# Transposes of gated retention tokens by pairs in one two-bank PSUM tile, with a new order around them and more products of ones at both ends

## The chip, the cores and the metric

The kernel runs on one core of a Trainium2 chip. The metric is the device time of one execution in microseconds (us). The kernel before was run three times: 1474.34, 1474.58 and 1475.74 us, median 1474.58. Lower is better.

## What is computed

The reference is one inference step of a decoder with two layers: layer 0 mixes tokens by a short gated convolution, layer 1 by multi-scale retention with four heads; each mixer is followed by a SwiGLU feed-forward layer, and a last RMS norm ends the step. There are 512 prompt tokens of one sequence and 32 sample tokens (8 sequences of 4), 544 in all, each of 1024 numbers, everything in fp32. The part that the change touches is retention:

```
z = x @ w_in                      # q, k (256 a head), v, g (512 a head)
q, k = rotary(q), rotary(k) / 16
per chunk: o = (q k^T * decay) v + (q S) * cross_w      # S: 256 x 512 state of a head
           S = S * chunk_decay + (k * state_w)^T v
o = (o - mean(o)) / sqrt(var(o) + eps) * gn_g           # per token and head
out = (silu(g) * o) @ w_out
```

and the last norm:

```
y = x / sqrt(mean(x * x) + eps) * final_norm
```

The outputs are y of both groups and the new convolution and retention states.

## The kernel before, in words

**Layout and precision.** Activations lie with features on the 128 partitions and the 544 tokens along the free dimension. Each fp32 operand is split into a high and a low part (xh and xl, wh and wl; ACT makes the high part at L185, DVE the low part at L186), and a product is the sum of three: high by high, low by high, high by low. `project` (L164 to 181, its matmul at L172) does this for one weight tile, eight k's of 128 and two halves of 272 tokens: 48 matmuls of 128x272. `mm3` (L160 to L162) does the same for the attention products.

**PSUM.** There are two pools. `psum()` hands out one of two tiles of two banks each (named mm in the profile), `bank()` one of four tiles of one bank (sm). A tile comes back to the pool when its last reader is done, and the instruction that takes it next waits for that reader. Dependencies are kept by tile.

**Order.** Instructions are issued to each engine in the order of the code, with due places set by `tc.issue_after(ins)`: what stands in that block goes behind the named instruction in the order. `last_product[0]` holds the last matmul of `project`, `mm3` or the sample products. Where two steps stand side by side a scheduler mixes them.

**A head of retention** (the loop over h, L1162 on). After values, gates, scores and states, for each of the four token tiles `inner` (L1043) makes the tile's attention output in a bank, from the middle state (mid by qk) and the scores (vh, vl by sh, sl), and `normalized` (L1031) brings it to group norm: statistics (L1036, L1037), the root by POOL (L219, L220), and yn = (pt − mean) · rs on DVE (L1040). `sample_outputs` (L1096, products at L1104) multiplies the sample queries by one of four pieces of the sample states S, loaded by `states_load` through SP's queue; `states_update` (L1109, four products at L1120 into two two-bank tiles, two DVE multiplications at L1125, then a store of S) brings the piece up to date. `gated` (L1060) transposes yn by four TensorE transposes (L1064) into a bank and multiplies the gate tile by it on DVE (L1067; L1071 for the sample tokens). `out_project` (L1128) splits the gated tokens into yh and yl and multiplies them by the output weights.

In heads 0 to 2, the rotated q and k of the next head are made meanwhile: `qk_project(h + 1, nxt, 1, 0)` and so on, each one `project` and its rotation on DVE (L866, L872 to L877). The order there is: the first of these projections; sample outputs of piece 3 and `inner` of tile 3; then `gated` of yn0 and yn1 (each with a bank of its own); normalisations of tile 2 and of the sample tokens (yns); the state update of piece 2; the second projection, with the state update of piece 3 and `gated` of yn2 inside it; normalisation of tile 3; `gated` of yns and of yn3; the last two projections and the output projection.

Head 3 has no next head. There two of the four gate projections are put late: `gate_project(3, 2)` with the state update of piece 2 inside, the sample outputs of piece 3, `gate_project(3, 3)` with the state update of piece 3 inside, then `gated` of yn0, yn1 and yn2 one behind the other, `inner` of tile 3, `gated` of yns, normalisation of tile 3 and the output projection, which takes `gated` of yn3 between two of its parts.

**The start.** While the first weights arrive, TensorE multiplies a tile of ones by itself (WARM = 7 times, L298).

**The last norm** (`final`, L698). The last three feed-forward output tiles are made for the first half of the tokens and then for the second; squares are summed (ACT at L210 and L214, DVE at L211 and L215), `scale` makes the means by three matmuls (L729), takes the root on POOL (L731) and spreads it over the partitions by three matmuls (L224). `gained` multiplies x by the norm's gains on ACT (L721), `out` multiplies by the spread root (L746 or POOL; R is a copy of it by ACT, L742) and stores. Three products of ones stand behind the sums of the second half (L765).

Of the kernel before, what the change touches and what calls it, by code (L numbers as in the profile page):

```python
# [9 lines left out]
AF = mybir.ActivationFunctionType  # L10
ALU = mybir.AluOpType

P = 128
D = 1024
KT = D // P
# [17 lines left out]
NVEC = 80  # L33
LATE = 3
LEAD = 3
WARM = 7

MADE = [0, 4, 2, 6, 3, 7, 1, 5]
RD = [(r, dt) for r in range(2) for dt in range(2)]
# [7 lines left out]
def hybrid_decode_kernel(ctx: ExitStack, tc: tile.TileContext, a: dict, o: dict):  # L47
    nc = tc.nc
# [26 lines left out]
    def bank():  # L75
        return ps.tile([P, 512], F32, tag="sm", name=nm("sm"), bufs=4)
# [16 lines left out]
    ident = cb[:, 544 : 544 + P]  # L93
    mean_w = cb[:, 672 : 672 + P]
# [19 lines left out]
    def g_fin(kt):  # L114
        return vec[:, 72 + kt : 73 + kt]
# [41 lines left out]
    last_product = [None]  # L157
# [64 lines left out]
    def spread(out, tt, lo, hi):  # L222

        return nc.tensor.matmul(  # L224
            out, rN[:, tt : tt + 1].to_broadcast([P, P]), ident[:, lo:hi], start=True, stop=True, skip_group_check=True
        )
# [471 lines left out]
    def final(ms, acts, group_weights, fp, tp):  # L698

        ah, al = acts  # L700
        ws = [group_weights(n, ms) for n in range(KT - LATE, KT)]

        sums = {}

        def products(hf):
            c = slice(hf * HT, (hf + 1) * HT)
            for n in range(KT - LATE, KT):
                wh, wl = ws[n - KT + LATE]
                pt = [None, None]
                pt[hf] = bank()  # L710
                project(pt, wh, wl, 0, ah, al, hfs=(hf,))
                nc.vector.tensor_add(x[n][:, c], x[n][:, c], half(pt, hf)[:, :HT])
                square_sum(n, tp, "gu", 4, c=c, add=nc.vector)
                yield

        def gained(hf):

            c = slice(hf * HT, (hf + 1) * HT)
            y = [fp.tile([P, 4, HT], F32, tag="f", name=nm("ya")), tp.tile([P, 4, HT], F32, tag="gu", name=nm("yb"))]
            for kt in range(KT):  # L720
                last_gain[0] = nc.scalar.activation(y[kt // 4][:, kt % 4, :], x[kt][:, c], AF.Copy, scale=g_fin(kt))  # L721
            return y

        def scale(hf):
            pt = bank()
            mq = pt[:, 496:499]
            for i, at in enumerate((0, P, HT - P)):
                cols = slice(hf * HT + at, hf * HT + at + P)
                last_sum[0] = nc.tensor.matmul(mq[:, i : i + 1], sqacc[:, cols], mean_w[:, 0:1], start=True, stop=True)  # L729
            nc.vector.tensor_scalar_add(rN[:, :3], mq, EPS)  # L730
            nc.gpsimd.tensor_tensor(rN[:, :3], rN[:, :3], expo[:, :3], op=ALU.pow)  # L731
            yield
            for i, (lo, hi) in enumerate(((0, P), (0, P), (3 * P - HT, P))):
                spread(pt[:, i * P : i * P + hi - lo], i, lo, hi)
            sums[hf] = pt[:, :HT]

        def out(hf, y, w):

            yy = y[w // 2][:, w % 2 * 2 : w % 2 * 2 + 2, :]
            if w == 0:  # L740
                with tc.issue_after(last_square[0].ins):
                    nc.scalar.activation(R[:, hf, :], sums[hf], AF.Copy)  # L742
                for i in range(2):
                    nc.gpsimd.tensor_tensor(yy[:, i, :], yy[:, i, :], R[:, hf, :], op=ALU.mult)
            else:
                nc.vector.tensor_mul(yy, yy, sums[hf].unsqueeze(1).to_broadcast([P, 2, HT]))  # L746
            q = nc.sync if w % 2 else nc.scalar
            q.dma_start(o["yT"][hf][:, 2 * w : 2 * w + 2], yy)

        last_gain, last_sum = [None], [None]  # L750
        drain(products(0))
        first, second = scale(0), products(1)
        next(second)
        next(first)
        y0 = gained(0)
        drain(second)
        drain(first)
        out(0, y0, 0)
        out(0, y0, 1)
        rest = scale(1)  # L760
        next(rest)
        with tc.issue_after(last_sum[0].ins):
            wm = bank()
            for _ in range(3):
                nc.tensor.matmul(wm[:, :P], ones, ones, start=True, stop=True)  # L765
        y1 = gained(1)
        out(0, y0, 2)
        out(0, y0, 3)
        drain(rest)
        for w in range(4):  # L770
            out(1, y1, w)
# [4 lines left out]
    with ExitStack() as c2:  # L776
# [37 lines left out]
        def token_tiles(tt):  # L814
            return slice(tt * P, (tt + 1) * P)
# [35 lines left out]
        def qk_project(h, st, which, dt, inside=None):  # L851

            wh, wl = load_piece(a["rtqk"][h, which * 2 + dt], KT * P)
            pt = [bank(), bank()] if inside else psum()
            if inside:
                project(pt, wh, wl, 0, xh, xl, last=False, ks=range(KP))
                inside()
                project(pt, wh, wl, 0, xh, xl, first=False, ks=range(KP, KT))
            else:
                project(pt, wh, wl, 0, xh, xl)  # L860
            qk_rotate(st, which, dt, pt)
# [195 lines left out]
                )  # L1057
            return pt

        def gated(h, st, yn, it):  # L1060

            pt = bank()
            for n in range(4):
                nc.tensor.transpose(pt[:, token_tiles(n)], yn[:, token_tiles(n)], ident)  # L1064
            if it < 4:
                gs = st["gate"][:, :, token_tiles(it)]
                nc.vector.tensor_mul(gs, gs, pt.rearrange("p (n t) -> p n t", n=4))  # L1067
            else:
                gs = st["gate"][:, :, SEQ:].rearrange("p n (g c) -> p n g c", g=4)
                ys = pt.rearrange("p (n g c) -> p n g c", n=4, g=4)[:, :, :, 0:8]  # L1070
                nc.vector.tensor_mul(gs, gs, ys)  # L1071

        def sample_scores(h, st):

# [87 lines left out]
        for h in range(NH):  # L1162
            more = h + 1 < NH
            value(h, st)
            st["S"] = {}
            for i in range(3):
                states_load(h, st, i)
            gate_project(h, st, 0)
            sample_operands(h, st)
            state(h, st, 0)  # L1170
            gate_project(h, st, 1)
            state(h, st, 1)
            for c in range(2):
                scores(h, st, c)
            if more:
                gate_project(h, st, 2)
                gate_project(h, st, 3)
            sample_outputs(h, st, 0)
            states_update(h, st, 0)
            states_load(h, st, 3)  # L1180
            yn0 = normalized(inner(h, st, 0))
            sample_outputs(h, st, 1)
            yn1 = normalized(inner(h, st, 1))
            states_update(h, st, 1)
            sample_outputs(h, st, 2)
            p2 = inner(h, st, 2)
            if more:
                nxt = qk_start(h + 1)
                for which in (1, 0):
                    qk_scale(nxt, which)  # L1190
                with tc.issue_after(last_product[0].ins):
                    qk_project(h + 1, nxt, 1, 0)
                sample_outputs(h, st, 3)
                p3 = inner(h, st, 3)
                with tc.issue_after(last_product[0].ins):
                    gated(h, st, yn0, 0)
                    gated(h, st, yn1, 1)
                yn2 = normalized(p2)
                yns = normalized(st["po"])
                states_update(h, st, 2)  # L1200

                def inside():
                    states_update(h, st, 3)
                    gated(h, st, yn2, 2)

                qk_project(h + 1, nxt, 1, 1, inside)
                yn3 = normalized(p3)
                gated(h, st, yns, 4)
                gated(h, st, yn3, 3)
                qk_project(h + 1, nxt, 0, 0)  # L1210
                qk_project(h + 1, nxt, 0, 1)
                out_project(h, st)
            else:
                yn2 = normalized(p2, "gt")
                gate_project(h, st, 2, lambda: states_update(h, st, 2))
                sample_outputs(h, st, 3)
                yns = normalized(st["po"], "rot1")
                gate_project(h, st, 3, lambda: states_update(h, st, 3))
                for it, yn in enumerate((yn0, yn1, yn2)):
                    gated(h, st, yn, it)  # L1220
                p3 = inner(h, st, 3)
                gated(h, st, yns, 4)
                yn3 = normalized(p3)
                out_project(h, st, [lambda: None, lambda: gated(h, st, yn3, 3)])
            st = nxt
# [121 lines left out]
```

## Time and profile before

| what | value |
|---|---|
| median of three runs | 1474.58 us (1474.34 to 1475.74) |
| the profiled execution's own time | 1474.22 us |
| span of its instructions | 1472.4 us |
| matmuls on TensorE | 11002 |
| DMA | 172.83 MB, mean 117 GB/s |
| mean granted clock of TensorE | 0.997 |

The profile is of one execution. Engines are PE (TensorE's matmuls), PEld (its weight loads, which lie beside PE), DVE (VectorE), ACT (ScalarE), POOL (GpSimd) and SP (SyncE, which issues most DMAs). A row of a time line has the start in us, the duration, the engine, the line of the kernel, the operation, output <- inputs by the program's names, the shape and the count (x4: four instructions taken together); in brackets stands how long the engine had been idle before, and what ended that. In the rows of waits, the numbers are the total in us, the number of times and the longest. fp32 matmuls (transposes, products of ones) leave two records each where the fp32r matmuls of the projections leave one; for transposes the profile shows one. The ends of matmuls are modelled, so distances are better read from start to start. The clock granted to TensorE is given as a share of full speed.

### The profile page before, as it was taken

What the parts mean: (1) busy time and instruction counts of PE and PEld (TensorE: products, weight loads), DVE (VectorE), ACT (ScalarE), POOL (GpSimd) and SP (SyncE); (2) the same over time, 40 slices, a digit from 0 to 9 for tenths busy, and PEclk for the clock granted to TensorE, in tenths of its full rate; (3) what the DMA queues carried; (4) which work ended last, traced back from release to release, by engine and by line L of the source; (5) the groups of instructions that cost most, each with busy time, mean ns of one, the idle gap of its engine ahead of it and who ended that gap; (6) DMA issues with size and microseconds to landing.
All of it is one profiled execution on the core that took longest, in us unless ns stands there. A gap on an engine that the chain in (4) does not pass through costs nothing.

```text
span 1472.4 us, 25982 instructions
## 1 busy us (share of the span) xinstructions
PE 1457.5 (99%) x11002; PEld 1388.6 (94%) x11002; DVE 921.2 (63%) x1397; ACT 572.4 (39%) x821; POOL 82.7 (6%) x107
## 2 busy tenths in 40 slices
PE   9999999999999999999999999999999999999997
PEld 9999999999999999897987988898799999999997
DVE  5645439847748647648545834844759847748645
ACT  5222355625525335242142224114265625525434
POOL 0100220000000003000000000000030000000002
PEclk9999999999999999999999999999999999999998
DMA  6222274232322326337235513714564232322322
GB/s 223 82 93 86 89 175 112 91 103 89 100 93 88 100 65 192 105 115 249 82 115 186 187 45 118 267 44 135 180 154 109 94 104 89 105 93 88 101 65 83
DMA packets 69748, 172.83 MB, mean 117 GB/s; under 512 B 6512, under 2 KB 23792, under 8 KB 69632
## 3 DMA queue, kind: packets, MB, share of 16 engines
q1 hardware_dynamic: 66576, 162.01, 33.5%
q0 software_dynamic: 2192, 7.94, 3.3%
q8 instruction: 86, 1.41, 0.4%
q10 hardware_dynamic: 864, 1.22, 0.2%
q14 instruction: 30, 0.25, 0.0%
HBM read 149.97 MB, written 21.18 MB: 116 GB/s over the span
## 4 chain that ended last, share of the span: by engine, by line
PE 95%; DVE 2%; DMA 2%; ACT 0%; POOL 0%; issue 0%; DVEq 0%; POOLq 0%; ACTq 0%; SPq 0%
PE mm L172 42%; PE sm L458 26%; PE sm L172 13%; PE sm L898 2%; PE sm L899 2%; PE sm L900 2%; PE sm L160 1%; PE sm L162 1%; PE sm L161 1%; DMA S<-in_rets_dram 1%; PE sm L1104 1%; DVE S L1125 1%; PE mm L905 1%; DVE yn L1040 0%; PE sm L224 0%; PE mm L1120 0%
## 5 line engine op out<-in xcount | busy, mean ns | idle before, releaser
L185 ACT ACTIVATE wh<-w 128x1024 fp32r<-128x1024 f32 (+4 forms) x215 | 209.9, 980 | 454.8 <-PE mm L172 269.4
L186 DVE TENSOR_TENSOR wl<-w,wh 128x1024 fp32r<-128x1024 f32 (+4 forms) x215 | 243.1, 1135 | 44.2 <-ACT wh L185 40.9
L172 PE MATMUL mm<-xh,wh 128*128 128x272 f32 x1060 | 221.7, 290 | 0.3 <-ACT wh L185 0.3
L172 PE MATMUL mm<-xl,wh 128*128 128x272 f32 x1060 | 219.5, 288 | 0.0
L172 PE MATMUL mm<-xh,wl 128*128 128x272 f32 x1060 | 219.5, 289 | 0.0
L172 PEld LDWEIGHTS mm<-xh,wh 128*128 128x128 f32 x1060 | 166.3, 189 | 5.4 <-DVE wl L186 3.4
L172 PEld LDWEIGHTS mm<-xl,wh 128*128 128x128 f32 x1060 | 166.6, 189 | 0.0
L458 PE MATMUL sm<-oh,wh 128*128 128x272 f32 x576 | 166.6, 289 | 0.0
L458 PE MATMUL sm<-oh,wl 128*128 128x272 f32 x576 | 166.5, 289 | 0.0
L458 PE MATMUL sm<-ol,wh 128*128 128x272 f32 x576 | 166.2, 289 | 0.0
L172 PEld LDWEIGHTS mm<-xh,wl 128*128 128x128 f32 x1060 | 165.7, 189 | 0.4
L266 DVE TENSOR_TENSOR x<-x,mm 128x544 f32<-128x544 f32 x85 | 61.2, 720 | 145.5 <-PE mm L172 145.5
L458 PE MATMUL sm<-oh,l 128*128 128x272 f32 x432 | 124.8, 289 | 0.0
L458 PE MATMUL sm<-ol,h 128*128 128x272 f32 x432 | 124.7, 289 | 0.0
L458 PE MATMUL sm<-oh,h 128*128 128x272 f32 x432 | 124.7, 289 | 0.0
L458 PEld LDWEIGHTS sm<-oh,wh 128*128 128x128 f32 x576 | 108.6, 189 | 0.6 <-ACT u L515 0.6
L458 PEld LDWEIGHTS sm<-oh,wl 128*128 128x128 f32 x576 | 108.7, 189 | 0.0
L458 PEld LDWEIGHTS sm<-ol,wh 128*128 128x128 f32 x576 | 108.5, 188 | 0.0
L186 DVE TENSOR_TENSOR l<-w,h 128x1024 fp32r<-128x1024 f32 x72 | 68.8, 956 | 55.5 <-ACT h L185 55.3
L172 PE MATMUL mm<-xh,f 128*128 128x272 f32 x576 | 99.3, 288 | 0.0
L172 PE MATMUL sm<-xh,wh 128*128 128x272 f32 x412 | 90.2, 292 | 0.7 <-DVE yn L1040 0.5
L172 PE MATMUL sm<-xh,wl 128*128 128x272 f32 x412 | 87.8, 288 | 0.0
(264 smaller groups left out, 2863.2 us busy)
## 6 DMA issues: line engine op xcount, KB each, us to landing
w<-in_ffgu_dram SPq DMA_DIRECT2D x88, 512.0 KB, 3.5
w<-in_ffdn_dram SPq DMA_DIRECT2D x96, 192.0 KB, 2.5
S<-in_rets_dram SPq DMA_DIRECT2D x16, 1024.0 KB, 7.1
out_rets_dram<-S SPq DMA_DIRECT2D x16, 1024.0 KB, 4.8
w<-in_cvin_dram SPq DMA_DIRECT2D x21, 512.0 KB, 3.5
w<-in_rtqk_dram SPq DMA_DIRECT2D x16, 512.0 KB, 3.7
w<-in_rtv_dram SPq DMA_DIRECT2D x16, 512.0 KB, 3.6
w<-in_rtg_dram SPq DMA_DIRECT2D x16, 512.0 KB, 3.9
```

The source lines that it names most:

```text
L160: nc.tensor.matmul(out, lh, rh, start=start, stop=False, skip_group_check=True)
L161: nc.tensor.matmul(out, lh, rl, start=False, stop=False, skip_group_check=True)
L162: last_product[0] = nc.tensor.matmul(out, ll, rh, start=False, stop=stop, skip_group_check=True)
L172: last_product[0] = nc.tensor.matmul(half(pt, hf)[:, :HT], w[:, c], act[k][:, hf * HT : (hf + 1) * HT], start=(first and k == ks[0] and i ...
L185: h = nc.scalar.activation(dh, src, AF.Copy)
L186: nc.vector.tensor_sub(dl, src, dh.bitcast(F32))
L266: last_residual[0] = nc.vector.tensor_add(xk, xk, p)
L458: nc.tensor.matmul(out, w[:, c], b[k][:, at, :], start=(first and k == 0 and i == 0), stop=(k == n - 1 and i == 2), skip_group_check=True,)
L898: nc.tensor.matmul(out, xh[kt][:, ts_], wh[:, cw], start=(kt == 0), stop=False)
L899: nc.tensor.matmul(out, xh[kt][:, ts_], wl[:, cw], start=False, stop=False)
L900: nc.tensor.matmul(out, xl[kt][:, ts_], wh[:, cw], start=False, stop=(kt == KT - 1))
L905: nc.tensor.matmul(pvs[g * NS : (g + 1) * NS, 0, :], xs[:, kt, :], raw[kt // 2][:, kt % 2 * DV : (kt % 2 + 1) * DV], start=(c == 1), stop= ...
```

## The change

1. `WARM` goes from 7 to 8.
2. `gated` can be given a tile. `gated_pair` takes one two-bank tile by `psum()` and lets two `gated` write its two halves. The transposes now also set `last_product[0]`.
3. Heads 0 to 2: `gated` of yn0 and yn1 become a pair and move ahead of the sample outputs of piece 3 and of `inner` of tile 3, right behind the first projection. `gated` of yns and yn3 become a pair.
4. Head 3: the sample outputs of piece 3 move, with the state update of piece 3, to the inside of the last gate projection; the normalisation of the sample tokens comes behind that projection; yn0 and yn1 become a pair, yn2 keeps a bank.
5. The last norm: four products of ones behind the spreads of the first half, the sums of the second half behind these, five products of ones (before: three) behind the sums. The last two gains of the second half are issued behind the last square.

```diff
-WARM = 7
+WARM = 8
...
             for kt in range(KT):
-                last_gain[0] = nc.scalar.activation(y[kt // 4][:, kt % 4, :], x[kt][:, c], AF.Copy, scale=g_fin(kt))
+                with tc.issue_after(last_square[0].ins) if hf and kt == KT - 2 else ExitStack():
+                    nc.scalar.activation(y[kt // 4][:, kt % 4, :], x[kt][:, c], AF.Copy, scale=g_fin(kt))
...
+        def idle(n, ins):
+
+            with tc.issue_after(ins):
+                wm = bank()
+                for _ in range(n):
+                    last_spread[0] = nc.tensor.matmul(wm[:, :P], ones, ones, start=True, stop=True)
...
+        idle(4, last_spread[0].ins)
         rest = scale(1)
-        next(rest)
-        with tc.issue_after(last_sum[0].ins):
-            wm = bank()
-            for _ in range(3):
-                nc.tensor.matmul(wm[:, :P], ones, ones, start=True, stop=True)
+        with tc.issue_after(last_spread[0].ins):
+            next(rest)
+        idle(5, last_sum[1].ins)
         y1 = gained(1)
...
-        def gated(h, st, yn, it):
+        def gated(h, st, yn, it, pt=None):
 
-            pt = bank()
+            pt = bank() if pt is None else pt
             for n in range(4):
-                nc.tensor.transpose(pt[:, token_tiles(n)], yn[:, token_tiles(n)], ident)
+                last_product[0] = nc.tensor.transpose(pt[:, token_tiles(n)], yn[:, token_tiles(n)], ident)
...
+        def gated_pair(h, st, *pair):
+            pt = psum()
+            for i, (yn, it) in enumerate(pair):
+                gated(h, st, yn, it, pt[:, i, :])
...
                     qk_project(h + 1, nxt, 1, 0)
+                with tc.issue_after(last_product[0].ins):
+                    gated_pair(h, st, (yn0, 0), (yn1, 1))
                 sample_outputs(h, st, 3)
                 p3 = inner(h, st, 3)
-                with tc.issue_after(last_product[0].ins):
-                    gated(h, st, yn0, 0)
-                    gated(h, st, yn1, 1)
...
-                gated(h, st, yns, 4)
-                gated(h, st, yn3, 3)
+                gated_pair(h, st, (yns, 4), (yn3, 3))
...
                 gate_project(h, st, 2, lambda: states_update(h, st, 2))
-                sample_outputs(h, st, 3)
+
+                def inside():
+                    sample_outputs(h, st, 3)
+                    states_update(h, st, 3)
+
+                gate_project(h, st, 3, inside)
                 yns = normalized(st["po"], "rot1")
-                gate_project(h, st, 3, lambda: states_update(h, st, 3))
-                for it, yn in enumerate((yn0, yn1, yn2)):
-                    gated(h, st, yn, it)
+                gated_pair(h, st, (yn0, 0), (yn1, 1))
+                gated(h, st, yn2, 2)
```

The order in which the instructions of the changed program stand on each engine: in heads 0 to 2 PE has, behind the first projection, the four transposes of yn0, five products of `inner` of tile 3, the four transposes of yn1, the four sample products of piece 3, the other seven products of `inner`, the four products of the state update of piece 2, 24 projection products, the four of piece 3, the transposes of yn2, 24 projection products, the transposes of yns, 19 projection products and the transposes of yn3. On DVE the gate multiplication by yn0 stands right behind the first rotation (L866), then the normalisation of tile 2 and the gate multiplication by yn1. PE has seven instructions more than before (10840 for 10833), all products of ones.

More of the change, by code (lines that the diff above doesn't have):

```diff
@@ L728, in scale @@
                 cols = slice(hf * HT + at, hf * HT + at + P)
-                last_sum[0] = nc.tensor.matmul(mq[:, i : i + 1], sqacc[:, cols], mean_w[:, 0:1], start=True, stop=True)
+                last_sum[hf] = nc.tensor.matmul(mq[:, i : i + 1], sqacc[:, cols], mean_w[:, 0:1], start=True, stop=True)
             nc.vector.tensor_scalar_add(rN[:, :3], mq, EPS)
@@ L733, in scale @@
             for i, (lo, hi) in enumerate(((0, P), (0, P), (3 * P - HT, P))):
-                spread(pt[:, i * P : i * P + hi - lo], i, lo, hi)
+                last_spread[0] = spread(pt[:, i * P : i * P + hi - lo], i, lo, hi)
             sums[hf] = pt[:, :HT]
@@ L748, in out @@
             q.dma_start(o["yT"][hf][:, 2 * w : 2 * w + 2], yy)
-        last_gain, last_sum = [None], [None]
+        last_sum, last_spread = {}, [None]
+        def idle(n, ins):
[3 more added lines that the diff above has]
+                    last_spread[0] = nc.tensor.matmul(wm[:, :P], ones, ones, start=True, stop=True)
         drain(products(0))
```

## The prediction

> **What bounds the kernel now.** I read the page first (busy times, then the chain that ended last), then PE's waits, then the time line of PE and DVE around the code that the change touches.
>
> ```profile
> span 1472.4 us, 25982 instructions
> PE 1457.5 (99%) x11002; PEld 1388.6 (94%) x11002; DVE 921.2 (63%) x1397; ACT 572.4 (39%) x821; POOL 82.7 (6%) x107
> PE 95%; DVE 2%; DMA 2%; ACT 0%; POOL 0%; issue 0%; DVEq 0%; POOLq 0%; ACTq 0%; SPq 0%
> ```
>
> TensorE (PE) is busy for 1457.5 of 1472.4 us and makes up 95% of the chain. The change removes no product of the model, so it can win only where PE stands still or runs at a lower clock, about 15 us. This view of PE's waits names such places:
>
> ```profile
> PE sm L1104 <- DMA S<-in_rets_dram: 1.6, 2, 1.0
> PE sm L1064 <- DVE gate L1067: 1.5, 3, 0.5
> PE sm L1064 <- DVE yn L1040: 1.4, 4, 0.4
> PE sm L729 <- DVE sqacc L211: 1.2, 2, 1.0
> PE sm L172 <- DVE yn L1040: 0.5, 3, 0.2
> ```
>
> (After the arrow the releaser; then the total in us, how often, the longest.) The transposes of gated tokens (L1064) and what follows them wait 1.5 + 1.4 + 0.5 = 3.4 us, the sample products (L1104) 1.6 us for their state's DMA, the last sums (L729) 1.2 us. The change aims at these; 1474.22 us is the profiled execution, 1.8 us of it outside the span.
>
> A 0.2% change is 2.95 us, about what a measurement of this kernel can tell from none. The shown runs' median, 1474.58, lies 0.36 above the profiled execution and their spread is 1.40; I add no correction for it.
>
> **Heads 0 to 2.** Head 0 on PE, then on DVE (start, duration, line; in brackets the idle time before and what ended it):
>
> ```profile
> 677.01 0.40 PE L160 MATMUL sm<-mid,qkh 128*128 128x512 f32 x1
> 677.25 0.39 PE L161 MATMUL sm<-mid,qkh 128*128 128x512 f32 x1
> ...
> 680.97 0.60 PE L1064 MATMUL sm<-cb,yn 128*128 128x128 f32 x4
> 681.49 0.51 PE L1120 MATMUL mm<-vs,kns 32*128 32x512 f32 x4
> 682.51 0.66 PE L1064 MATMUL sm<-cb,yn 128*128 128x128 f32 x4 [0.51 <-DVE gate L1067]
> 683.32 0.37 PE L172 MATMUL sm<-xh,wh 128*128 128x272 f32 x1 [0.15 <-DVE yn L1040]
> ...
> 686.51 0.51 PE L1120 MATMUL mm<-vs,kns 32*128 32x512 f32 x4
> 686.95 0.39 PE L172 MATMUL sm<-xh,wh 128*128 128x272 f32 x1
> 687.18 0.60 PE L1064 MATMUL sm<-cb,yn 128*128 128x128 f32 x4
> 687.53 0.37 PE L172 MATMUL sm<-xh,wh 128*128 128x272 f32 x1
> ...
> 690.49 0.60 PE L1064 MATMUL sm<-cb,yn 128*128 128x128 f32 x4
> 690.85 0.50 PE L172 MATMUL mm<-xh,wh 128*128 128x272 f32 x2
> ...
> 691.86 0.66 PE L1064 MATMUL sm<-cb,yn 128*128 128x128 f32 x4 [0.40 <-DVE yn L1040]
> ```
>
> ```profile
> 677.22 0.72 DVE L866 TENSOR_TENSOR rot<-mm,gt 128x544 f32<-128x544 f32 x1 [4.02 <-PE mm L172]
> ...
> 681.78 0.67 DVE L1067 TENSOR_TENSOR gate<-gate,sm 128x512 f32<-128x512 f32 x1
> 682.37 0.81 DVE L1040 TENSOR_SCALAR yn<-sm,mv,rs 128x512 f32<-128x512 f32 x1
> ...
> 683.90 1.19 DVE L1125 SCALAR_TENSOR_TENSOR S<-S,mm 128x1024 f32<-128x1024 f32 x1
> ...
> 685.07 1.21 DVE L1125 SCALAR_TENSOR_TENSOR S<-S,mm 128x1024 f32<-128x1024 f32 x1
> ...
> 691.00 0.81 DVE L1040 TENSOR_SCALAR yn<-sm,mv,rs 128x512 f32<-128x512 f32 x1 [0.72 <-POOL rs L220]
> ```
>
> Ends of matmuls are modelled, so I take start to start. Four transposes ahead of products take 687.53 − 687.18 = 0.35, four L1120 products 686.95 − 686.51 = 0.44. What goes:
> - Transposes of yn0 ahead of L1120 take 681.49 − 680.97 = 0.52, ahead of products 0.35: 0.17 won.
> - L1120 to the transposes of yn1, 682.51 − 681.49 = 1.02, of which 0.44 is work: 0.58 won. That is the second transposes' wait for a one-bank tile (the four are taken), which the first gate multiplication (681.78 + 0.67 = 682.45) gives back.
> - Transposes of yn1 to the next product, 683.32 − 682.51 = 0.81 against 0.35: 0.46 won; that product's bank was waiting for yn2's normalisation (682.37 + 0.81).
> - Transposes of yn3, 691.86 − 690.85 = 1.01 for three products. The 23 between 687.53 and 690.49 take 0.129 each, three 0.39; with 0.08, by estimate, for the restart behind transposes 0.47 is work, 0.54 won. In the changed order 19 products stand ahead of them, not 3. They start about 692.3, yn3 ends about 692.1.
>
> Together 1.75 us. What is added: the transposes of yn0 and yn1 go into one two-bank tile, and the program's dependency is by tile: yn1's must wait until DVE has read yn0's. Behind them in PE's queue stand L1104, seven products of the inner part and L1120. Yn0's transposes now start at 677.01, five products of 0.235 follow, so yn1's are due at 677.01 + 0.35 + 1.26 = 678.62. In the changed order the gate multiplication stands right behind L866, so it begins at 677.22 + 0.72 = 677.94 and ends at 678.61: no wait, and nothing to spare. I take 0; its bounds are 0 and 0.35 (half of one such multiplication late).
>
> Second, the two L1120 of the last sample state use two-bank tiles that the previous update's L1125 has to empty. L1120 of state 2 moves to about 681.7, its two L1125 end about 685.6, and the second pair of L1120 is due at about 685.3: 0.25 us of new wait, with yn2's transposes and the projection behind it. Bounds 0 and 0.5. The split of a weight on DVE (L186) falls behind them, to about 685.6; its product is due at about 696, so ten microseconds cover it. Ahead of L1104 there now stand 0.35 + 1.26 + 0.35 = 1.96 us in place of eight products of 0.235, 1.88; it comes no later than 0.1, so the S load's wait in head 1 stays (1.0, the longest of L1104's row). On SP the output weights' load passes behind one store of S and the next head's S load behind one weight; neither is due within 10 us. POOL's order is unchanged; ACT's splits of the gated tokens come earlier with the gates.
>
> So 1.75 − 0.25 = 1.5 a head, **−4.5 us** for three; bounds 1.1 and 1.75 a head, −3.3 and −5.3.
>
> **Head 3** has no next head to fill with.
>
> ```profile
> 1047.66 1.04 PE L1104 MATMUL sm<-S,qm 128*8 128x512 f32 x8 [0.64 <-DMA S<-in_rets_dram]
> 1054.97 1.47 PE L1064 MATMUL sm<-cb,yn 128*128 128x128 f32 x12
> 1059.80 0.52 PE L172 MATMUL mm<-yh,wh 128*128 128x272 f32 x2
> 1060.63 0.40 PE L172 MATMUL mm<-yl,wh 128*128 128x272 f32 x1 [0.31 <-DVE rs L219]
> 1062.38 0.52 PE L1064 MATMUL sm<-cb,yn 128*128 128x128 f32 x3 [0.23 <-DVE yn L1040]
> ```
>
> The sample products move behind half a gate projection, about 2 us later, so their wait (0.64, some 0.75 start to start) goes; the store of S and the update move with them, and the S slots are not needed again. But the state's two L1125 (2.4 us of DVE by the rows above) now come ahead of yns' normalisation. That frees the bank for the last inner part, which I put at 1055.5 where PE is ready at 1054.9: 0.6 lost. The first product of y then needs the split of all first-half tokens, and yn1's gate comes after the statistics of p3: about 1060.75, 0.95 later than 1059.80, of which the old waits behind it (0.31 and about 0.4 ahead of 1062.38) come back. Transposes of yn3 stay at about 1062.3, bound by DVE, but four fewer products (4 × 0.125) were done ahead. So what decides is the four products, 0.5, less some 0.2 of waits behind them that this leaves out. The sum is **+0.3 us**: the DMA's 0.75 is spent on DVE's queue. Bounds −0.8 (only the DMA wait goes) and +1.0 (both new waits, nothing back).
>
> **The tail and the start.**
>
> ```profile
> 1.06 3.35 PE L298 MATMUL sm<-ones 128*128 128x128 f32 x14 [1.06 <-DVE expo L100]
> 4.72 1.01 PE L172 MATMUL mm<-xh,wh 128*128 128x272 f32 x2 [0.31 <-ACT wh L185]
> ...
> 1460.42 0.74 PE L224 MATMUL sm<-cb,rN 128*128 128x128 f32 x6
> 1462.17 0.83 PE L729 MATMUL sm<-cb,sqacc 128*128 128x1 f32 x6 [1.01 <-DVE sqacc L211]
> 1462.87 1.44 PE L765 MATMUL sm<-ones 128*128 128x128 f32 x6
> 1464.34 1.47 PE L224 MATMUL sm<-cb,rN 128*128 128x128 f32 x6
> ...
> 1463.10:1472.00 8.90, 2.67 (x12) 2.27 (x11) 3.40 (x6) 0.40 (x1) 2.67 (x4) 0.50 0.66 250
> ```
>
> (The last row is the table by stretch: PE, PEld, DVE, ACT and POOL busy, then the granted clock.) At 1463.1 the clock falls to 0.50, and the last spreads (L224) take 1.47 instead of 0.74. The four new products of ones, eight records of 0.12 (0.74 over six), fill the idle time from 1461.1 to 1462.1, when the sums' input is there; five behind the sums reach to about 1464. If the clock then holds, the spreads end 0.73 earlier. With the last two gains put behind the last square on ACT, that square starts one activation earlier but still behind two: 0.08. I take **−0.8**; bounds 0 (the clock falls anyway) and −0.9.
>
> The Trainium skill, "TensorE: Matmul & The Clock Gate", section "What's actually happening", has the clock halved after an idle window of about 3.4 us. By that the 1.01 us of idle here should not have closed it; the row of 0.50 says that it did, and the measurement decides. By the page alone, the tail's gain would be 0.08, and the sum 0.7 higher.
>
> At the start an eighth product of ones adds two records of 0.24 (3.35 over 14) and ends about 4.63, before the first real product at 4.72: no cost. If the clock opens a little earlier, the weights' loads limit the gain: **−0.1**, bounds −0.2 and +0.3 (if the records reached past 4.72).
>
> Sum: 1474.22 − 4.5 + 0.3 − 0.8 − 0.1 = **1469.1 us**.
>
> **Rivals.**
> 1. The waits only move. Each head keeps one DVE wait of about 0.5 to 0.6 more than I count (yn1's transposes behind yn0's gate, yn3's because yn3 is only 0.2 ahead). For: DVE does the same work. Against: the walk above leaves yn1 no wait. Three heads give 3 × (−1.5 + 0.6) = −2.7, head 3 +0.8, tail and start 0: 1472.3, within 0.2%. It also covers the case that the two-bank tile doesn't do what it is for, the second transposes waiting as long as before. Chance 0.18.
> 2. The clock closes once in the middle. Head 3's new wait of up to 1.4 us stands in one stretch; half clock for one window of 3.4 us costs 1.7: 1470.8. Against: head 1's wait of 1.0 us left the clock (the last but two) at 1.00:
>
> ```profile
> 803.40:806.80 3.40, 2.44 (x14) 1.43 (x16) 3.16 (x4) 1.01 (x1) 0.00 (x0) 1.00 0.99 359
> ```
>
> The Trainium skill, same page, section "A second HAM failure mode: psum-queue depth-cycling", tells of clocks lost to many short waits between groups; by that rule this could also befall the heads, and the time would be this rival's. No row of before shows it. Chance 0.10.
> 3. Slower. The place is DVE's queue at yn0's gate multiplication. In before it runs at 681.78 to 682.45. If it kept that place, yn1's transposes would hold PE from 678.62 to 682.45, with L1104 and all behind: 3.8 lost a head against 1.5 won, 3 × 2.3 = 6.9, less 0.5 for head 3, tail and start: 1480.6. It decides against the change from a gate that ends later than 678.62 + 1.5 = 680.1. Against it stands the order, with the gate right behind L866. Chance 0.08.
>
> **How the numbers follow.** The forecast has the rest, 0.64, its own range 1467.3 to 1470.9. Faster: 0.64 + 0.10 = 0.74; same 0.18; slower 0.08. The range goes from the sum of the good bounds (−5.3 − 0.8 − 0.9 − 0.2: 1467.0) to just above rival 1's time, 1472.5, and leaves out rival 3 and some of rival 1, 2 in 10.
>
> **What would show it.** Right: the rows of L1064 waiting for gate and yn shrink from 2.9 to under 1; a new row of about 0.25 × 3 where L1120's successor waits for L1125; L1104's DMA row down to the 1.0 of head 1; the y products of head 3 waiting over 1 us; the clock at 1.00 through the last spreads, of about 0.74. Wrong: transposes of yn1 waiting over 0.3 in a head, a clock row under 1.00 before the tail, or head 3 over 1 us slower.

## The result and the profile after

Ten executions of the changed kernel took 1470.80 us in the median (1469.78 to 1472.37), ten of the kernel before 1474.96 (1474.34 to 1475.91). The ratio is 0.9973, with a 95% interval of 0.9963 to 0.9982: 4.2 us faster, between 2.7 and 5.5. On another chip the same pair gave 0.9979 (0.9970 to 0.9987). The prediction was 1469.1 in a range of 1467.0 to 1472.5, so 5.1 us faster than the profiled execution of before.

The page after shows the same picture as before, with a span shorter by 3.9 us:

```profile
span 1468.5 us, 26015 instructions
PE 1457.3 (99%) x11016; PEld 1388.8 (95%) x11016; DVE 920.5 (63%) x1397; ACT 572.4 (39%) x821; POOL 84.3 (6%) x107
```

PE has 14 records more (the products of ones) and is busy for as long: what has gone is time in which it stood still. PE's waits after (releaser; total, times, longest):

```profile
PE mm L172 <- ACT yh L185: 1.2, 1, 1.2
PE sm L298 <- DVE expo L100: 1.1, 1, 1.1
PE sm L1117 <- DMA S<-in_rets_dram: 0.8, 1, 0.8
PE sm L160 <- DVE yn L1048: 0.4, 1, 0.4
PE sm L172 <- DVE rs L219: 0.3, 1, 0.3
PE sm L1072 <- DVE yn L1048: 0.2, 1, 0.2
PE sm L730 <- DVE sqacc L211: 0.2, 1, 0.2
```

Lines below the edits have moved: L1072 here is L1064 of before, L1075 is L1067, L1048 is L1040, L1117 is L1104, L1133 is L1120, L1138 is L1125, L730 is L729 and L758 is L765. The rows of transposes waiting for the gate (1.5) and for yn (1.4) have shrunk to one of 0.2. Two rows are new, both in head 3: the first product of yh (1.2) and the last inner part (0.4).

Where the time went is read from the starts of the same instruction in both traces; the last column is the change of the shift, which is what that stretch won:

| first of | before | after | shift | won in the stretch before it |
|---|---|---|---|---|
| sample products, head 0 | 662.52 | 661.62 | −0.90 | start −0.95, then +0.05 |
| output products, head 0 | 703.94 | 702.22 | −1.72 | head 0: −0.8 |
| output products, head 1 | 831.36 | 828.40 | −2.96 | head 1: −1.2 |
| output products, head 2 | 957.76 | 953.90 | −3.86 | head 2: −0.9 |
| output products, head 3, the last | 1085.46 | 1082.42 | −3.04 | head 3: **+0.8** |
| spreads of the first half | 1460.42 | 1457.30 | −3.12 | last feed-forward layer −0.1 |
| end of the last spreads | 1465.81 | 1461.94 | −3.87 | tail −0.75 |

Three heads won 3.0 us and not 4.5, head 3 lost 0.8 and not 0.3, the tail won what was forecast, and the start shows 0.95 that no step of the prediction had. In head 0 after:

```profile
677.70 0.62 PE L1072 MATMUL mm<-cb,yn 128*128 128x128 f32 x4
678.45 1.04 PE L1117 MATMUL sm<-S,qm 128*8 128x512 f32 x8
...
681.24 0.50 PE L1133 MATMUL mm<-vs,kns 32*128 32x512 f32 x4
...
684.86 0.78 PE L1133 MATMUL mm<-vs,kns 32*128 32x512 f32 x4
685.57 0.66 PE L1072 MATMUL sm<-cb,yn 128*128 128x128 f32 x4
685.98 0.50 PE L172 MATMUL sm<-xh,wh 128*128 128x272 f32 x2
...
691.75 0.29 PE L172 MATMUL mm<-xh,wh 128*128 128x272 f32 x1
692.11 0.66 PE L1072 MATMUL mm<-cb,yn 128*128 128x128 f32 x4
```

Read start to start: the transposes of yn1 begin at 677.70 without a wait (five products after yn0's), but L1117 follows after 0.75. In head 2 of experiment 3, where the load had landed 0.24 before its use, the same step takes 0.55: 0.2 of it is the wait for the load of S. The second set of L1133 takes 684.86 to 685.57, 0.71, where the first takes 0.43: 0.28, the new wait for DVE's L1138. The transposes of yn3 come 0.36 behind one product that takes 0.12: 0.24 of wait that the prediction didn't have. DVE shows why:

```profile
685.00 0.18 DVE L1045 BATCH_NORM_AGGREGATE mv<-bst 128x2 f32<-128x6 f32 x1
685.09 1.19 DVE L186 TENSOR_TENSOR wl<-w,wh 128x1024 fp32r<-128x1024 f32 x1
686.20 2.35 DVE L1138 SCALAR_TENSOR_TENSOR S<-S,mm 128x1024 f32<-128x1024 f32 x2
688.46 0.68 DVE L1075 TENSOR_TENSOR gate<-gate,sm 128x512 f32<-128x512 f32 x1
689.13 0.79 DVE L874 TENSOR_TENSOR rot<-sm,gt 128x272 f32<-128x272 f32 x2
689.84 0.14 DVE L219 TENSOR_SCALAR rs<-mv 128x1 f32<-128x1 f32 x1
689.90 0.28 DVE L1079 TENSOR_TENSOR gate<-gate,mm 128x128 f32<-128x128 f32 x1
690.10 0.72 DVE L882 TENSOR_TENSOR rt<-rot,sqlast 128x544 f32<-128x544 f32 x1
691.25 0.81 DVE L1048 TENSOR_SCALAR yn<-sm,mv,rs 128x512 f32<-128x512 f32 x1 [0.43 <-POOL rs L220]
```

The mean and variance of tile 3 are there at 685.2, but the addition of epsilon, 0.14 us long, stands in DVE's queue behind 4.6 us of other work. Only then can POOL take the root, and yn3 is ready at 692.06. The root itself is the other half: it takes 1.08 us here, and 0.54 in the same place of before.

```profile
690.13 1.08 POOL L220 TENSOR_TENSOR rs<-rs,expo 128x1 f32<-128x1 f32 x1 [7.34 <-DVE rs L219]
```

With 0.54 it would be done at 690.67, and DVE is busy with L882 until 690.82; by this estimate yn3 would be ready at 691.63, ahead of 691.87, where its transposes are due, and the wait of 0.24 took both, the late addition and the long root. In the fourteen profiles the root of a token tile takes over 0.75 us 21 times, each time beside a multiplication of the rotation like L882, and less in the 259 others. Why is not shown.

### The profile page after: what moved, and what is told of

Read it like the earlier page. It is cut to its first block, busy times and chain, and to the rows that moved or that the text cites. A ratio compares the mean times of both kernels' runs of the same rounds, so it can differ in the third digit from the quotient of the medians.

```text
span 1468.5 us, 26015 instructions
## 1 busy us (share of the span) xinstructions
PE 1457.3 (99%) x11016; PEld 1388.8 (95%) x11016; DVE 920.5 (63%) x1397; ACT 572.4 (39%) x821; POOL 84.3 (6%) x107
## 4 chain that ended last, share of the span: by engine, by line
PE 93%; DVE 4%; DMA 2%; POOL 1%; ACT 0%; issue 0%; DVEq 0%; POOLq 0%; ACTq 0%; SPq 0%
PE mm L172 41%; PE sm L458 26%; PE sm L172 13%; PE sm L906 2%; PE sm L907 2%; PE sm L908 2%; DMA S<-in_rets_dram 2%; DVE S L1138 1%; PE sm L160 1%; PE sm L162 1%; PE sm L161 1%; PE sm L1117 1%; PE mm L913 1%; DVE yn L1048 0%; DVE wl L186 0%
```

## The experiments

All were timed in five rounds beside the kernel before. The short diffs are against the kernel named.

**1. The eighth product of ones alone** (against before):

```diff
-WARM = 7
+WARM = 8
```

> The kernel before with the eighth product of ones at the start and nothing else. Theory (the start's 0.95 us in the profile after is the moment at which the clock happened to open, 7.0 us in place of 9.0, and not the product): within 0.3 us of before. Rival (the eighth product fills the stretch that decides whether the clock opens one window earlier): 0.9 us faster, first products of the input projection at full speed from about 7 us or earlier in its profile.

Measured: 1473.74 us (1473.17 to 1474.75) beside 1474.25, ratio 0.9996 (0.9987 to 1.0005): not told from no change. Its profile shows the early stretch 0.9 us earlier, as the rival had it (first spreads at 31.80 for 32.71), but so does experiment 4's, with seven products (31.73).

**2. Heads 0 to 2 alone** (before, with change 3 and the helpers of change 2).

> The kernel before with the pairs and the new order of heads 0 to 2 alone; head 3, start and tail as before. Theory (three heads won 0.80, 1.22 and 0.90): 2.9 us faster, each head's step to its output projection as in the profile after. Rival (the prediction's 1.5 a head, hidden in the profile after by a late DMA of one execution): 4.5 us faster.

Measured: 1470.36 us, ratio 0.9976 (0.9967 to 0.9985), 3.5 us faster; the profile gives the heads −1.0, −1.7 and −0.8, 3.5 together. Between the two expectations; the heads alone carry nearly the whole result, and the step of one head varies by half a microsecond between executions, with the landing of S.

**3. The changed kernel with head 3 in its old order** (after, with the else branch of before).

> The changed kernel with head 3 in the order of before. Theory (head 3's new order loses 0.8 by two DVE waits): 0.8 us faster than the changed kernel, 4.9 faster than before. Rival (the loss of head 3 is only where the profile puts the S load's wait that would come anyway): same as the changed kernel.

Measured: 1470.16 us beside 1474.25, ratio 0.9973 (0.9963 to 0.9983). By the times this can't be told from the changed kernel; the two profiles tell it. Head 3 in its old order takes as long as in before, within 0.1, the new one 0.8 longer, and in this run's waits the rows of yh and of the last inner part are gone, while the S load makes three waits, head 3's again among them:

```profile
PE sm L1117 <- DMA S<-in_rets_dram: 1.8, 3, 0.7
```

**4. The tail alone** (before, with change 5).

> The kernel before with the changed tail alone: four products of ones behind the first spreads, five behind the sums, two gains behind the last square. Theory: 0.75 us faster, last spreads in 0.74 to 0.85 in place of 1.47, clock at 1.00 until they are done. Rival (where the clock falls is luck of the window, whatever the ones): same time within 0.2 us, last spreads at 1.4 again.

Measured: 1473.60 us, ratio 0.9996 (0.9987 to 1.0005), 0.6 by the medians, and from the first spreads to the end of the last 0.74 in the profile. What tells it from chance is the granted clock of every execution: 0.998 or 0.999 in all eleven of this kernel (0.999 in eight), 0.997 or 0.998 in all 29 of the kernel before on the same chip, and 0.997 or 0.998 in all eleven of experiment 1. Luck of the window there is too: in experiment 2, with the old tail, the clock fell a little later and the last spreads took 0.84, and so in experiment 6.

**5. The new place without the tile** (experiment 2, with banks):

```diff
-            pt = psum()
-            for i, (yn, it) in enumerate(pair):
-                gated(h, st, yn, it, pt[:, i, :])
+            for yn, it in pair:
+                gated(h, st, yn, it)
```

> Heads 0 to 2 in the new order, but each set of transposes in a bank of its own, head 3, start and tail as before. Theory (order and two-bank tile are both needed): two of the four banks are taken in front of the inner part of tile 3, which then waits about 0.9 us a head for the gate multiplication by yn0; the waits of yn1's transposes go, yn3's stays: within 1 us of before. Rival (the new place alone wins, in whatever tile): 3.5 us faster, as the heads-only kernel.

Measured: 1476.00 us beside 1474.94, ratio 1.0005 (0.9996 to 1.0014), within 1 us as the theory had it. PE's waits show it: the inner part (L160) waits for the gate, 0.5 a head where the theory had 0.9, and yn3's transposes wait as in before.

```profile
PE sm L1108 <- DMA S<-in_rets_dram: 2.5, 2, 1.7
PE sm L160 <- DVE gate L1067: 1.6, 3, 0.5
PE sm L1064 <- DVE yn L1040: 1.4, 4, 0.5
```

**6. The tile without the new place** (experiment 2, with the pair behind the inner part):

```diff
-                with tc.issue_after(last_product[0].ins):
-                    gated_pair(h, st, (yn0, 0), (yn1, 1))
                 sample_outputs(h, st, 3)
                 p3 = inner(h, st, 3)
+                with tc.issue_after(last_product[0].ins):
+                    gated_pair(h, st, (yn0, 0), (yn1, 1))
```

> The pairs in two-bank tiles, but the pair of yn0 and yn1 behind the inner part of tile 3, where the transposes stood before; head 3, start and tail as before. Theory (the tile ends the shortage of banks, but takes one of the two tiles that the state updates need): the 0.58 and 0.46 a head go, a wait of 0.3 to 0.6 for the gate multiplication by yn1 comes at the state update, yn3's wait goes in part: 1.5 to 2.5 us faster. Rival (the place does it): same as before within 0.5 us.

Measured: 1477.35 us beside 1474.94, ratio 1.0014 (1.0005 to 1.0023): 2 us **slower**, against both expectations. The waits of the transposes are gone, but the last projection before the output products now waits in each head, here in head 2, on PE, DVE and ACT:

```profile
954.41 0.41 PE L172 MATMUL mm<-xh,wl 128*128 128x272 f32 x2
955.76 0.49 PE L172 MATMUL mm<-xh,wh 128*128 128x272 f32 x2 [0.93 <-ACT wh L185]
```

```profile
954.93 0.68 DVE L1067 TENSOR_TENSOR gate<-gate,mm 128x512 f32<-128x512 f32 x1
```

The row names ACT, which ended a weight's high part at about the same moment; but in the program's order the weight of this product was split one projection earlier, and what the product takes is the two-bank tile of the second pair, which the gate multiplication by yn3 (954.93 + 0.68 = 955.61) gives back. In this order yn3 was normalised behind the steps of the rotation, and so a tile held for the later of its two halves kept the projection waiting for 1.1 us. In the changed kernel the same multiplication ends at 694.56 and the projection that takes the tile starts at 696.24: there are 1.7 us to spare, a margin that the prediction did not look at.

The held tile is the second pair's, so the time alone does not tell what the first pair is worth in its old place. The profile does. Counted from a head's first sample product, less the step into the last sample products (which holds the wait for S), the transposes of yns, where the second pair begins, come after 27.95 us in head 0, for 27.64 in before: 0.3 later, though the first pair's transposes no longer wait. The scheduler had put the eight products of the two state updates in four groups of two, and no longer in two of four.

**7. The store of state piece 1 behind the load of piece 3** (experiment 3, `last_state` being the load of a state piece):

```diff
-            nc.sync.dma_start(rets_out[r, h, dt], S)
+            with tc.issue_after(last_state[0].ins) if i == 1 else ExitStack():
+                nc.sync.dma_start(rets_out[r, h, dt], S)
```

> The changed kernel with head 3 as before, and the store of state piece 1 put behind the load of piece 3 in SP's queue. Theory (that store, on its way from 670 to 675 us, is what makes the load land at 678.4): the load lands 2 to 3 us earlier in each head, the sample products wait for no DMA (0.29, 0.93, 0.23 and 0.8 in head 3): 2.0 us faster than without it, some 6 faster than before. Rival (the load is as slow for the weights that move beside it): landing within 0.5 us of the old one, time the same.

Measured: 1471.28 us beside 1474.94, ratio 0.9974 (0.9964 to 0.9984): no gain on experiment 3. The loads of piece 3 did land sooner, 6.6 to 6.7 us after their issue for 7.7 to 8.7 in experiment 3, and the sample products' wait did fall, to 1.0 us in three, but the scheduler answered the new store with another order on DVE, yn3 late again, and the wait of experiment 6 came three times:

```profile
PE mm L172 <- ACT wh L185: 2.8, 3, 0.9
PE sm L1119 <- DMA S<-in_rets_dram: 1.0, 3, 0.6
```

**8. The statistics of tile 3 early** (experiment 3; `normalized` cut in two, the first part called ahead of the second projection):

```diff
+                by3 = statistics(p3)
                 qk_project(h + 1, nxt, 1, 1, inside)
-                yn3 = normalized(p3)
+                yn3 = normalized(p3, by=by3)
```

> The changed kernel with head 3 as before, and the statistics of tile 3 issued ahead of the second projection, which puts the small addition of epsilon on DVE ahead of the last state update instead of behind it, the gate multiplication and the rotation. Theory (that place in DVE's queue is the 0.24 us wait of yn3's transposes): three waits go, 0.7 us faster than without it, 4.8 faster than before. Rival (POOL's root or the normalisation itself is late): the wait stays over 0.15 in each head.

Measured: 1469.90 us beside 1474.94, ratio 0.9961 (0.9947 to 0.9974). The transposes of yn3 follow the product in front of them after 0.12, with no wait; heads 0 to 2 win 3.35 for 2.85 in experiment 3. The interval overlaps that of experiment 3, so the time alone does not show the 0.5.

```profile
693.45 0.29 PE L172 MATMUL mm<-xh,wh 128*128 128x272 f32 x1
693.57 0.60 PE L1077 MATMUL mm<-cb,yn 128*128 128x128 f32 x4
```

**9. Both, 7 and 8 together.**

> The changed kernel with head 3 as before, the statistics of tile 3 early and the store of state piece 1 behind the load of piece 3. In this order yn3's normalisation stands on DVE ahead of the last rotation steps again. Theory (the later store helps the load by 0.4 to 2 us and what it lost before was only that yn3's gate multiplication came late and held the two-bank tile that the last projection needs, 1.1 us a head): no such wait of 1.1, sample products wait for under 1 us in all: 1 to 2 us faster than with early statistics alone, 6 to 7 faster than before. Rival (the later store delays weights on SP's queue whatever DVE does): the waits of 1.1 stay, 4 faster than before.

Measured: 1467.72 us (1467.57 to 1468.25) beside 1475.00, ratio 0.9954 (0.9941 to 0.9968): 6.8 us faster than before, with experiment 12 the fastest of all. The S loads (16 in either kernel) land earlier, experiment 3 first, this one second:

```profile
DMA to landing us min/median/max: 5.5/8.1/9.8
```

```profile
DMA to landing us min/median/max: 4.8/6.5/8.7
```

PE's waits in it:

```profile
PE sm L1124 <- DMA S<-in_rets_dram: 0.8, 2, 0.4
PE mm L172 <- ACT wh L185: 0.6, 2, 0.4
```

The waits of 1.1 are gone with yn3 in its early place, which is what the theory of the held tile asks for; the heads win 0.9, 2.4 and 1.1, head 3 another 0.6.

**10. The second pair in banks** (experiment 8, `gated` of yns and of yn3 in a bank each).

> The changed kernel with head 3 as before and the statistics of tile 3 early, and the transposes of the sample tokens and of yn3 in a bank each in place of the second pair. Theory (these transposes wait for the normalisation, not for a bank; the second pair brings nothing): within 0.5 us of the same kernel with the second pair, 5 faster than before. Rival (the second pair's tile is part of the gain): a wait of the projection or of the transposes for a gate multiplication comes back, 0.5 or more a head, 3.5 faster than before.

Measured: 1469.81 us beside 1475.00, ratio 0.9966 (0.9954 to 0.9979), for 0.9961 with the second pair: the theory's side, though the interval does not exclude a small gain of the pair. By the profile the heads win 3.6, no less than with it, and without the wait for S a head takes the same with either (39.9, in the table below). The gain is the first pair's.

**11. The changed kernel once more.**

> The changed kernel once more, beside the other two on one chip. All theories: 4.2 us faster than before, as measured, within the interval of 0.9963 to 0.9982.

Measured: 1471.09 us (1470.24 to 1474.01) beside 1475.00, ratio 0.9979 (0.9970 to 0.9987). Its profile shows something new, in the table by stretch (PE busy first, the granted clock third from the end):

```profile
1055.92:1059.34 3.42, 2.04 (x13) 1.40 (x12) 2.93 (x9) 1.39 (x4) 0.71 (x1) 1.00 0.20 74
1059.34:1062.76 3.42, 3.42 (x17) 3.38 (x16) 1.43 (x4) 0.17 (x1) 0.00 (x0) 0.50 0.00 0
1062.76:1066.18 3.42, 3.42 (x29) 3.42 (x29) 2.20 (x5) 1.22 (x4) 0.00 (x0) 1.00 0.00 0
```

That is rival 2 of the prediction, in head 3: after a stretch with 1.4 us of idle PE the clock is halved for one stretch of 3.4 us. Head 3 lost 2.1 here in place of 0.8. Three of the eleven executions had a granted clock of 0.997, and they took 1472.17, 1472.44 and 1474.01, the slowest of the eleven; the others had 0.998 or 0.999.

**12. Experiment 9 with seven products of ones.**

```diff
-WARM = 8
+WARM = 7
```

> The fastest kernel so far (head 3 as before, early statistics, later store) with seven products of ones at the start in place of eight. Theory (the start's gain is where the clock's window falls, not the product): 0.9954 of before as with eight, within 0.0004. Rival (the eighth product wins what the profile after showed at the start): 0.9 us slower than with eight, 0.9960.

Measured: 1467.50 us beside 1474.47, ratio 0.9954 (0.9941 to 0.9968), as with eight. The first spreads stand at 31.65 for 32.71 in before, 1.06 earlier, with seven products: the start's gain in the profile after was not the product's.

## Why the prediction was right, and where its sizes were wrong

**Heads 0 to 2: the mechanism right, the size not** (3.0 in the profile after, 2.5 and 3.5 in two others, for 4.5). The two waits named, of yn1's transposes for a bank and of the next product for yn2, did go, and experiments 5 and 6 show that it takes the tile and the place together: either alone gave nothing, or cost 2 us. The added wait at the second L1120 was put at 0.25 and measured 0.28; yn1's transposes were said not to wait, and did not.

The kernels differ most clearly in what a head takes without its wait for S, from its first sample product to its first output product, less the step into the last sample products:

| profiles | us, heads 0 to 2 |
|---|---|
| before, experiments 1 and 4 | 41.04 to 41.09 |
| experiment 5, the place alone | 41.31, 42.26 (the clock closed), 41.30 |
| experiment 6, the tile alone | 41.96 to 41.97 |
| after (both profiles), experiments 2 and 3 | 40.16 to 40.23 |
| experiment 7, later store | 40.91 to 40.92 |
| experiments 8 and 10, early statistics | 39.88 to 39.92 |
| experiments 9 and 12, both | 39.73 to 39.77 |

The step left out takes 0.33 without a wait in before's order and 0.20 in the new one, so the new order wins 0.9 + 0.1 = 1.0 a head and not 1.5. Two terms of the sum were mis-sized, and one wait that it left alone moved between the heads:
- The 0.17 of "transposes of yn0 ahead of L1120" was not won. In the changed order products of the inner part stand ahead of L1133: 681.24 − 680.91 (the start of the product before it) is 0.33 for a product of 0.23, so the same price of 0.1 is paid there, and the product behind yn0's transposes pays another 0.08; and the transposes of yn1 take 0.55 ahead of the sample products, where 0.35 was counted. A price between neighbours moved with them.
- The transposes of yn3 "start about 692.3, yn3 ends about 692.1" took the normalisation's time from before's order. In the changed order the small L219 stands behind two L1138, the gate and the rotation, the root behind it takes twice as long, and PE waits 0.24 a head. Experiment 8, with L219 early and a root of 0.54 again, took that wait away.
- L1104's load was left as it was, for head 1 alone. The load lands within a microsecond of PE's arrival in all three heads, and by the steps of 0.20 and 0.33 the wait was 0.2, 0.8 and 0.1, for 0, 1.0 and 0.1 in before. In sum that is the same: the load makes the heads differ, and is no part of the shortfall.

**Head 3: the sign right, the size 0.8 for 0.3.** Both waits came: the last inner part starts 0.97 behind the start of transposes that take 0.35 (1050.83), so 0.6 late as forecast, and the first product of yh waits 1.16 by its row:

```profile
1051.80 0.50 PE L160 MATMUL sm<-mid,qkh 128*128 128x512 f32 x1 [0.37 <-DVE yn L1048]
...
1055.19 0.60 PE L1072 MATMUL sm<-cb,yn 128*128 128x128 f32 x4
1056.95 0.52 PE L172 MATMUL mm<-yh,wh 128*128 128x272 f32 x2 [1.16 <-ACT yh L185]
...
1058.67 0.55 PE L1072 MATMUL sm<-cb,yn 128*128 128x128 f32 x3 [0.23 <-DVE yn L1048]
```

The step that failed is the waits that were to come back. The 0.31 did: the first product of yl follows that of yh after 0.47, for 0.83. The 0.4 ahead of yn3's transposes did not: from the product in front of them they take 0.51 in both profiles. The transposes, said to "stay at about 1062.3", which on the shift of head 2 would be 1058.5, came at 1058.67. So the four products, 0.5, were lost whole, with 0.15 on top and some 0.2 in small steps.

**The tail: right** (0.75 for 0.8). The ones fill the idle time, the sums start 0.12 earlier on the common shift, and the last spreads take 0.84 where before's took 1.47:

```profile
1457.30 0.74 PE L224 MATMUL sm<-cb,rN 128*128 128x128 f32 x6
1457.88 1.14 PE L758 MATMUL sm<-ones 128*128 128x128 f32 x8
1458.93 0.83 PE L730 MATMUL sm<-cb,sqacc 128*128 128x1 f32 x6
1459.62 1.36 PE L758 MATMUL sm<-ones 128*128 128x128 f32 x10
1461.10 0.84 PE L224 MATMUL sm<-cb,rN 128*128 128x128 f32 x6
```

**The start: 0.1 was as good as one can say.** The 0.95 of this profile hangs on when the clock opened, at 6.84 us here and at 9.00 in before, and on when the next weights landed: in experiment 2 the clock opened at 4.99, and nothing was won, because PE then waited 1.18 us for a weight that landed at 8.02 (7.25 here). Experiments 1 and 12 leave nothing measurable for the product itself. The forecast's end of the ones at 4.63 does not follow from its row, 1.06 + 3.35 + 0.48 = 4.89; they reach 4.84 here, and the first product of the model starts at 4.76 for 4.72, which costs nothing to speak of.

**The rivals.** The waits did move in part: the heads gave back 1.5 of the forecast 4.5, near the 1.8 that rival 1 charged them, but by other ways than it named, and the tail kept its gain. Rival 2's closed clock came in one of the two profiles, in head 3, where it was placed; it cost 1.3 there (2.1 for 0.8), for 1.7 forecast. Rival 3's place, the gate multiplication by yn0 late on DVE, did not occur: it ran at 676.93, right behind the rotation. But its kind of wait, a gate multiplication late in DVE's queue that holds a tile, is what made experiment 6 slower, with yn3 in place of yn0.

The profile after ends 1.3 us above the forecast: 1.5 in the heads and 0.5 in head 3, less 0.85 at the start that no step had forecast. That part is luck.

Not settled: how much of the 4.2 us is head 3's loss. The profiles say 0.8, and 2.1 where the clock closed; the times of experiment 3 do not separate it.

## What to carry to other kernels

A two-bank tile for two results ends a shortage of banks, but it is held until the later result has been read; so find, before using it, who takes that tile next and how late the second reader may be. When products are moved to hide a wait, walk the small instructions too, with what runs beside them: an addition of 0.14 us behind 4.6 us in a queue, and a root of 1.08 us in place of 0.54, were what the next step waited for here. And when a load lands about when its reader arrives, take its wait out before comparing two profiles: here it was anything from 0 to 1.7 us, by head and by execution.

## What the runs showed of the hardware

The clock gate acts on a grid of 3.413 us: the clock is open from 9.00 to 1463.08 us in before and from 6.84 to 1464.33 after, which is 426 and 427 times that. In the same place of head 3, a grid stretch with PE busy for 2.25 of 3.41 us left the clock open in the profile after, and one with 2.04 (above) closed it in the next:

```profile
1054.73:1058.14 3.41, 2.25 (x16) 1.84 (x16) 2.92 (x8) 1.39 (x4) 0.72 (x1) 1.00 0.41 148
```

In experiment 5 a stretch with 1.56, through the 1.7 us wait for S in head 1, closed it too:

```profile
803.90:807.32 3.42, 1.56 (x11) 1.00 (x9) 2.64 (x4) 1.03 (x1) 0.00 (x0) 1.00 1.04 340
807.32:810.73 3.41, 3.06 (x11) 1.17 (x12) 1.10 (x2) 0.00 (x0) 0.00 (x0) 0.50 0.36 138
```

So waits of 1.2 to 1.7 us were enough in these two stretches of the grid; where the grid falls differs between executions, and that is part of the spread of the times. The busy time of a stretch alone does not decide it. Over the sums of the tail, this stretch of before closed the clock:

```profile
1459.66:1463.08 3.42, 2.41 (x22) 2.31 (x21) 1.96 (x4) 2.67 (x7) 1.08 (x2) 1.00 0.00 0
```

This one of experiment 2, as busy, left it open:

```profile
1455.66:1459.07 3.41, 2.39 (x21) 2.29 (x20) 2.17 (x5) 2.74 (x8) 0.52 (x1) 1.00 0.00 0
```

And in experiment 12 the clock was still at 1.00 behind a stretch with 1.95 (from 1457.01 to 1460.42). What else counts is not shown.

The Trainium skill, "TensorE: Matmul & The Clock Gate", section "What's actually happening", has a free-running window of 3413 ns, with which the grid of 3.413 us agrees. It has the clock halved after an idle window; here a window that was 40% idle was enough once (2.04 of 3.42 us busy), and the measurement decides.
